# A hand-ordered opening with four projection tiles, and modulation dot products moved out of the gate stage, in an encoder-layer kernel

## The chip, the cores and the metric

The kernel runs on one core of a Trainium2 chip. A core has five engines, each with its own queue, which it works off in order: TensorE (PE in the profile) multiplies matrices into PSUM banks, VectorE (DVE), ScalarE (ACT) and GpSimd (POOL) work on tiles in SBUF, and SyncE (SP) issues most DMAs here. An instruction that waits for a semaphore holds up everything behind it on its own engine. The metric is the device time of one execution in microseconds; lower is better.

## The reference

One layer of an encoder over 1024 tokens of width 1024, in fp32, with one batch element. What is computed:

```python
mod = cond @ w_ada[l] + b_ada[l]                     # cond = silu(c); 6 x 1024 columns
sh1, sc1, g1, sh2, sc2, g2 = jnp.split(mod, 6, axis=-1)
h = modulate(rms_norm(x, norm_mix_g[l]), sh1, sc1)
proj = h @ w_in[l]
q_a, k_a, v_a, qk_m, v_m, o_m, gates = jnp.split(proj, splits, axis=-1)
y_attn = axial_gqa_attention(q_a, k_a, v_a, q_norm_g[l], k_norm_g[l], tables)
y_mem = bidirectional_mlstm(qk_m, v_m, o_m, gates, conv_w[l], conv_b[l], gate_b[l], mlstm_norm_g[l])
mix = jnp.concatenate([y_attn, y_mem], axis=-1) @ w_out[l]
x = x + g1[:, None, :] * mix
h = modulate(rms_norm(x, norm_ffn_g[l]), sh2, sc2)
ffn = (jax.nn.silu(h @ w_gate[l]) * (h @ w_up[l])) @ w_down[l]
x = x + g2[:, None, :] * ffn
```

and a last RMS norm. The attention has 8 query and 2 key heads, the mLSTM 4 heads that run over the sequence in both directions.

## The kernel before

Everything is held transposed: 8 tiles of 128 features by 1024 tokens, in two halves of 512 tokens. Each large product is made of three fp32r matmuls (`mm3`, L297): both factors are split into a high and a low part, and high x high, high x low and low x high are added up. So each weight piece needs a high part (ACT, `whi`) and a low part (POOL, `wlo`), and the input h its `hh` and `hl`.

The stages, in order of time:

1. **Opening.** c is loaded, broadcast to 128 partitions by its DMA, and put through silu (`load_cond`, L364). x is squared and summed (`sum_up`), two matmuls against a tile of ones (L553) give the mean square, and `rstd_steps` takes the root. The modulation `mod` is found in rows of 128: row j of 48 is the dot product of a 128 x 1024 tile of `w_ada` with cond, one DVE instruction (L96, `ada<-ada,cond`) over a tile that a DMA of 512 KB brings. Rows 0 to 7 are the shift and 8 to 15 the scale of the first norm, so the opening needs 16 of them: block k of h needs rows k and 8 + k (`h_steps`). The first three projection tiles (k, v, and the first pair of query heads) are accumulated block by block as h appears. Matmuls of `con` with ones (WARM0 = 9 ahead of the sums, WARM = 6 behind them) are there as well; their result is not used.
2. **Gate stage.** The remaining projections are a list of units, IN (L48): "q" query tiles, "f" tiles of the mLSTM's convolved q and k, "t" chunks with v, o and the gates. `t0` makes the gates; `gate_steps` then computes the mLSTM's decays in a chain of DVE and ACT steps with three visits to TensorE: transposes of the gate rows (`rows`), transposes into columns (`columns`), and one small matmul (`spread`). `rope_steps` (queries and keys) also visits TensorE once per tile, for the squares' sums (`squares`).
3. **Attention** (`scores`, `turned`, `values`), with what is left of IN in the gaps.
4. **mLSTM heads** (`states`, `front`, `back`, `ends`), with the rest of IN and then the output projection (MIX) in the gaps.
5. **Output projection, FFN.**

The order of the instructions on each engine is fixed when the program is built. `Clock` (`ck`) plays the kernel through with estimated costs; a step is emitted at the moment that it would become ready, and a stream of TensorE work is taken when the clock says that its inputs are there (`ck.streams`). `ck.chain` is a row of dependent steps. On the chip each engine then takes its queue in order, whatever the real times.

The other dot products, rows 16 to 47, are made in halves of 512 columns by `ada_late` (64 of them): one load of 256 KB, one DVE instruction. It keeps two tiles (`ahead=2`): the next load waits until the dot before the last one has read its tile. Rows 16 to 39 (48 halves) are to be done by the end of the attention, the last 16 halves during the heads, where a loop makes those that are missing as soon as the units of IN have run out:

```python
        ck.streams(mem, [un], stop=lambda: un.wait is None and all(f.done for v in vo_ok for f in v))
        while not summed:
            ck.need(*adas[-2:])
            ada_late(64)
```

In the gate stage `ready` (L1926) makes up to one half per microsecond, in the attention `scores` one per query block.

## Time and profile before

| | us |
|---|---|
| time, median of 3 runs (lowest, highest) | 1414.26 (1409.74, 1415.05) |
| the profiled execution: its time, its span | 1413.09, 1411.3 |
| busy: TensorE, VectorE, ScalarE, GpSimd | 1304.2, 1074.1, 662.9, 695.8 |
| first projection matmul of the opening | 36.97 |
| first matmul of `t0` (the opening's tiles are done) | 90.91 |
| first score matmul (the attention begins) | 206.24 |
| last `av` matmul (the attention ends), start | 509.3 |
| last transpose of an mLSTM head's output, start | 675.74 |

Times inside the execution are microseconds from the start of the span. L96 is the line of a helper that emits all instructions that `Clock` knows of, and L303 that of the DMA helper; such instructions are told apart by their tiles, `out<-in`. In a timeline row stand the start, the duration, the engine, the line, the operation, the tiles and shapes, and in brackets the idle time of the engine just before, with what ended it. A row of waits gives the total, the number and the longest.

### The profile page before, as it was taken

To read this page: it belongs to the slowest core of one execution; us is meant where nothing else is said; L and a number is where in the kernel's file an instruction comes from. 1 tells how busy PE (TensorE), PEld (TensorE's weight loads), DVE (VectorE), ACT (ScalarE), POOL (GpSimd) and SP (SyncE) were. 2 spreads that over 40 slices of the span, in tenths; PEclk is the share of its full clock that TensorE was granted. 3 is DMA by queue.
4 is the path that set the end of the run, shared out by engine and by line. 5 is a ranking of instruction groups with operands and counts; after the bars stand their busy time and mean duration, and the time that the engine had idled before them with its cause. 6 is when DMAs were issued, how large, how long until landed. Compare 5 with 4: busy or idle time off the path is not lost.

```text
span 1411.3 us, 19469 instructions
## 1 busy us (share of the span) xinstructions
PE 1304.2 (92%) x6594; PEld 1075.1 (76%) x6602; DVE 1074.1 (76%) x1590; ACT 662.9 (47%) x1194; POOL 695.8 (49%) x565
## 2 busy tenths in 40 slices
PE   5789798999999989899996899999999999989997
PEld 2578677889877979777774688888888887767887
DVE  6947979987788848768599886676666654998866
ACT  5454316676666655454575333233333333444462
POOL 5555554545344426687405454545445445545542
PEclk8899999999999999999997899999999999989999
DMA  7536462322122146563551342323322248823324
GB/s 283 168 118 205 132 180 79 101 83 64 38 57 77 34 137 209 180 213 118 192 194 60 101 138 95 107 99 111 113 94 85 83 164 322 297 82 103 92 64 153
DMA packets 103172, 184.39 MB, mean 131 GB/s; under 512 B 11297, under 2 KB 32673, under 8 KB 103073
## 3 DMA queue, kind: packets, MB, share of 16 engines
q1 hardware_dynamic: 89968, 161.06, 35.6%
q10 hardware_dynamic: 13104, 22.10, 4.2%
q8 instruction: 52, 0.85, 0.2%
q14 instruction: 48, 0.39, 0.1%
HBM read 136.19 MB, written 43.25 MB: 127 GB/s over the span
## 4 chain that ended last, share of the span: by engine, by line
PE 58%; DVE 21%; DMA 7%; issue 5%; ACT 4%; POOL 3%; SPq 1%; DVEq 0%; ACTq 0%; POOLq 0%
PE acc L299 14%; PE acc L300 14%; PE acc L298 14%; DVE x L96 3%; DVE ada L96 3%; DVE sst L96 3%; PE av L1029 3%; DMA wst<-act_d 2%; PE T L1010 2%; DVE PT L96 2%; DVE y L96 2%; PE S L978 2%; PE acct L298 1%; PE acct L300 1%; PE acct L299 1%
## 5 line engine op out<-in xcount | busy, mean ns | idle before, releaser
L96 POOL TENSOR_TENSOR wlo<-wst,whi 128x512 fp32r<-128x512 f32 (+2 forms) x190 | 271.0, 1432 | 293.6 <-ACT whi L96 284.3
L96 ACT ACTIVATE whi<-wst 128x512 fp32r<-128x512 f32 (+2 forms) x219 | 131.5, 605 | 131.2 <-POOL wlo L96 25.3
L96 POOL TENSOR_SCALAR P<-P,sst 128x1024 f32<-128x1024 f32 x64 | 88.8, 1391 | 143.7 <-DVE sst L96 114.9
L299 PE MATMUL acc<-x,whi 128*128 128x512 f32 x352 | 140.8, 400 | 6.1 <-DVE x L96 6.1
L96 POOL TENSOR_TENSOR wlo<-wr,whi 128x512 fp32r<-128x512 f32 x60 | 82.3, 1372 | 87.2 <-ACT whi L96 76.7
L298 PE MATMUL acc<-hh,whi 128*128 128x512 f32 x224 | 98.0, 438 | 12.7 <-ACT hh L96 10.2
L96 ACT ACTIVATE P<-S,sst,colq 128x1024 f32<-128x1024 f32 x64 | 77.2, 1207 | 52.4 <-DVE sst L96 49.5
L299 PE MATMUL acc<-hl,whi 128*128 128x512 f32 x224 | 93.1, 416 | 8.4 <-POOL hl L96 4.7
L298 PE MATMUL acc<-whi,wch 128*128 128x512 f32 x244 | 97.2, 398 | 3.9 <-ACT wch L96 3.9
L300 PE MATMUL acc<-whi,wcl 128*128 128x512 f32 x244 | 97.2, 398 | 2.8 <-DVE wcl L96 2.8
L299 PE MATMUL acc<-wlo,wch 128*128 128x512 f32 x244 | 97.5, 399 | 0.8 <-POOL wlo L96 0.7
L96 DVE SCALAR_TENSOR_TENSOR ada<-ada,cond 128x512 f32<-128x512 f32 (+1 forms) x79 | 81.7, 1042 | 18.3 <-DMA ada<-in_w_ada_dram 12.7
L300 PE MATMUL acc<-hh,wlo 128*128 128x512 f32 x224 | 92.0, 411 | 0.0
L96 DVE TENSOR_TENSOR sg<-acc,sg 128x512 f32<-128x512 f32 x67 | 45.4, 687 | 59.9 <-PE acc L300 59.5
L96 ACT ACTIVATE whi<-wr 128x512 fp32r<-128x512 f32 x60 | 37.9, 632 | 111.3 <-DVE wr L96 52.0
L96 ACT ACTIVATE PT<-T 128x512 fp32r<-128x512 f32 x128 | 71.4, 597 | 39.3 <-PE T L1010 38.6
L96 DVE TENSOR_TENSOR PT<-T,PT 128x512 fp32r<-128x512 f32 x128 | 82.8, 681 | 8.0 <-ACT PT L96 7.9
L299 PEld LDWEIGHTS acc<-x,whi 128*128 128x128 f32 x352 | 66.9, 190 | 22.9 <-DVE x L96 7.9
L298 PE MATMUL acct<-whi,hh 128*128 128x256 f32 (+1 forms) x256 | 79.5, 311 | 2.6 <-ACT xp L96 1.2
L1010 PE MATMUL T<-con,P 128*128 128x128 f32 x512 | 71.0, 278 | 9.8 <-DVE PT L96 7.1
L96 DVE TENSOR_TENSOR wcl<-wd,wch 128x512 fp32r<-128x512 f32 x50 | 50.9, 1031 | 38.0 <-ACT wch L96 28.8
L96 DVE TENSOR_REDUCE sst<-S 128x1 f32<-128x1024 f32 x64 | 77.6, 1213 | 2.4 <-PE S L978 2.2
(457 smaller groups left out, 3807.5 us busy)
## 6 DMA issues: line engine op xcount, KB each, us to landing
wr<-in_w_gu_dram SPq DMA_DIRECT2D x66, 256.0 KB, 2.7
ada<-in_w_ada_dram SPq DMA_DIRECT2D x64, 256.0 KB, 3.4
wd<-in_w_d_dram SPq DMA_DIRECT2D x22, 512.0 KB, 6.6
wst<-in_w_gu_dram SPq DMA_DIRECT2D x34, 256.0 KB, 3.1
wst<-act_d SPq DMA_DIRECT2D x33, 256.0 KB, 4.7
ada<-in_w_ada_dram SPq DMA_DIRECT2D x16, 512.0 KB, 5.5
wst<-in_w_o_dram SPq DMA_DIRECT2D x32, 256.0 KB, 3.7
act_d<-sg ACTq DMA_DIRECT2D x31, 256.0 KB, 2.2
```

The costliest lines, as they stand in the source:

```text
L96: return fn(*args, **kw)
L298: nc.tensor.matmul(acc, w[0], x[0], start=first, stop=False)
L299: nc.tensor.matmul(acc, w[0], x[1], start=False, stop=False)
L300: nc.tensor.matmul(acc, w[1], x[0], start=False, stop=last)
L978: nc.tensor.matmul(sp[:, halves(n)], qs[:, j * P:(j + 1) * P], k2[g][m][:, halves(n)], start=m == 0, stop=m == 1)
L1010: nc.tensor.transpose(tp[:, k], Pt[q][:, (4 * b + k) * P:(4 * b + k + 1) * P], ident)
L1029: nc.tensor.matmul(av, va[:, k, h // 4], PT[it][m][:, k], start=(k, m) == (0, 0), stop=(k, m) == (NJ - 1, 1))
```

## The change

- **Opening.** c is loaded as one row into a zeroed tile (`crow`), put through silu as one row, and broadcast by two matmuls with ones. The squares are taken on full tiles, added in pairs on DVE, and summed by eight matmuls. From `dot(8)` on, DVE, ACT and POOL instructions are written out in a fixed order, not left to the clock. POOL's part is only the low halves of weights; all low halves of h are on DVE. Four tiles are made (NT0 = 4, with the second query pair), whose eight weight pieces are loaded into four staging tiles more (`spare`, in the place of the keys). The last block goes tile by tile, so that the first tile is complete first. Then IN has no ("q", 1).
- **Dot products.** `ready` makes none, so none lies between the opening and the attention. By the end of the attention 32 halves are made instead of 48, and 32 instead of 16 fall to the heads; rows 32 to 39 and `sc2` move there with them.
- **Pauses.** `later(dt)` holds a chain back by dt in the planner's time: 2.5 ahead of `squares`, 6.0 ahead of `columns`, 5.0 ahead of `spread`. TensorE gets other work ahead of these steps.

```diff
-WARM = 6
-WARM0 = 9
-POOLED = (0,)
+WARM = 5
+WARM0 = 3
+NT0 = 4
-IN = ([("t", 0), ("q", 1), ("q", 2), ("q", 3), ("f", 0), ("f", 4), ("f", 1), ("f", 5), ("t", 2), ("f", 2), ("f", 6),
+IN = ([("t", 0), ("q", 2), ("q", 3), ("f", 0), ("f", 4), ("f", 1), ("f", 5), ("t", 2), ("f", 2), ("f", 6),
...
+        gp.memset(crow, 0.0)
+        nc.sync.dma_start(crow[0:1], c)
+        for k in range(KT):
+            nc.sync.dma_start(x_t[k], xT[k])
...
+        for j in (8, 0):
+            ada_load(j)
+        for f in range(NT0):
+            first_load(0, f)
+        for j in (9, 1, 10):
+            ada_load(j)
+        nc.sync.dma_start(con, cons)
+        for f in range(NT0):
+            first_load(1, f)
...
+        ac.activation(crow[0:1], crow[0:1], AF.Silu)
...
+        for n in range(NH):
+            nc.tensor.matmul(cb[n], ones, crow[:, halves(n)], start=True, stop=True)
...
+        dot(8)
+        gain(0)
+        root_v(0)
+        root_y(0)
+        ac.activation(msp[0], ry[0], AF.Square)
+        first_hi(0, 0)
+        first_lo(0, 0, gp)
+        dot(0)
+        shift(0)
...
+        def prepare(k):
+
+            if k + 1 < KT:
+                if k > 1:
+                    ada_load(9 + k)
+                ada_load(k + 1)
+            dot(8 + k)
+            gain(k)
+            dot(k)
+            shift(k)
             for n in range(NH):
...
+                xr(k, n)
+                h_hi_of(k, n)
+            for n in range(NH):
+                h_lo_of(k, n)
+            if k < 5:
+                first_hi(1, k - 1)
+                first_lo(1, k - 1, gp)
...
+        def later(dt):
+
+            def wait():
+                ck.fin = ck.now + dt
+            return wait
...
-            ck.chain(0.0, lambda: evac(0), lambda: evac(1), swap, squares)
+            ck.chain(0.0, lambda: evac(0), lambda: evac(1), swap, later(2.5), squares)
...
-                     lambda: exps(0), lambda: exps(1), state, lambda: exps(2),
+                     lambda: exps(0), lambda: exps(1), state, lambda: exps(2), later(6.0),
                      *[lambda i=i, b=b: columns(i, b) for i in range(2) for b in range(2)],
-                     lambda: dve.tensor_scalar(cols[:, :, 1], cols[:, :, 1], QK, None, op0=OP.mult), decay, spread,
+                     lambda: dve.tensor_scalar(cols[:, :, 1], cols[:, :, 1], QK, None, op0=OP.mult), decay, later(5.0), spread,
...
-        def ada_late(last=48, ahead=2):
+        def ada_late(last=32, ahead=2):
...
-                mod_sum(40, 48)
+                mod_sum(32, 48)
+                dve.scalar_tensor_tensor(sc2, mod[:, 32:40], 1.0, V("norm_ffn_g", 0, KT), op0=OP.add, op1=OP.mult)
...
-        t_ada = [0.0]
-
         def ready():
-            if ck.t > t_ada[0]:
-                ada_late()
-                t_ada[0] = ck.t + 1.0
             return rope_ok[3].done and gates_ok.done and not open_sum[0]
...
-        while len(adas) < 48:
+        while len(adas) < 32:
             ck.need(*adas[-2:])
             ada_late()
...
-        mod_sum(16, 40)
+        mod_sum(16, 32)
```

How this moves instructions is seen in the built programs. On DVE in the opening, one block of h (`x` is the tile of the block, `sq` the root of its half, `sc` the scale, `hh` and `hl` the high and low part of h). Before, for block 3:

```order
L96 TENSOR_TENSOR mod<-modacc,vec 128x1 x2
L96 SCALAR_TENSOR_TENSOR sc_343<-mod,vec 128x1
L96 TENSOR_TENSOR x_242<-x_242,sq 128x512
L96 SCALAR_TENSOR_TENSOR ada,modacc<-ada,cond 128x1024
L96 TENSOR_TENSOR x_242<-x_242,sq 128x512
L96 SCALAR_TENSOR_TENSOR ada,modacc<-ada,cond 128x1024 x2
```

and after the change:

```order
L546 SCALAR_TENSOR_TENSOR ada,modacc<-ada,cond 128x1024
L556 SCALAR_TENSOR_TENSOR sc_270<-modacc,b_271,vec 128x1
L546 SCALAR_TENSOR_TENSOR ada,modacc<-ada,cond 128x1024
L553 TENSOR_TENSOR mod<-modacc,vec 128x1
L609 SCALAR_TENSOR_TENSOR x_233<-x_233,sc_270,sq 128x512 x2
L615 SCALAR_TENSOR_TENSOR hl_215<-x_233,mod,hh_207 128x512 x2
```

A block's two dots now stand ahead of its own steps, the scaling is in the first of them, and the two low parts, which POOL made, have come to DVE.

On DVE after the attention's last `avt`, where the heads begin (`Cs` are the states, `W` the weights of a pair of chunks, `U` and `tr` PSUM banks). Before:

```order
L96 TENSOR_TENSOR mod<-modacc,vec 128x24
L96 TENSOR_TENSOR mod<-mod,modacc 128x24
L96 SCALAR_TENSOR_TENSOR sc_5007<-mod,vec 128x8
L96 SCALAR_TENSOR_TENSOR ada,modacc<-ada,cond 128x512 x3
L96 SCALAR_TENSOR_TENSOR Cs<-Cs,dec,U 128x130 x2
L96 SCALAR_TENSOR_TENSOR W<-tr,W 128x256 x2
L96 SCALAR_TENSOR_TENSOR ada,modacc<-ada,cond 128x512
L96 SCALAR_TENSOR_TENSOR Cs<-Cs,dec,U 128x130 x2
L96 SCALAR_TENSOR_TENSOR W<-tr,W 128x256 x2
L96 SCALAR_TENSOR_TENSOR ada,modacc<-ada,cond 128x512 x2
L96 SCALAR_TENSOR_TENSOR Cs<-Cs,dec,U 128x130 x3
```

and after the change:

```order
L96 SCALAR_TENSOR_TENSOR ada,modacc<-ada,cond 128x512 x2
L96 SCALAR_TENSOR_TENSOR Cs<-Cs,dec,U 128x130 x2
L96 SCALAR_TENSOR_TENSOR W<-tr,W 128x256 x2
L96 SCALAR_TENSOR_TENSOR ada,modacc<-ada,cond 128x512 x2
L96 SCALAR_TENSOR_TENSOR Cs<-Cs,dec,U 128x130
L96 SCALAR_TENSOR_TENSOR ada,modacc<-ada,cond 128x512 x28
L96 TENSOR_TENSOR mod<-modacc,vec 128x16
L96 TENSOR_TENSOR mod<-mod,modacc 128x16
L96 SCALAR_TENSOR_TENSOR sc_5133<-mod,vec 128x8
L96 SCALAR_TENSOR_TENSOR Cs<-Cs,dec,U 128x130
L96 SCALAR_TENSOR_TENSOR W<-tr,W 128x256 x2
```

The units of IN run out soon after the attention (264 chunk matmuls were left to the heads before, 108 are now), the loop quoted above then makes all dots that are missing, and 28 of them stand together between the third and the fourth state update.

Their loads stand together on SP as well (`mq` is a piece of the mLSTM's q, `wst` a weight piece, `x` a piece of the residual). Before, at the same place:

```order
L303 DMA wst<-in_w_o_dram 128x512
L303 DMA v_d_94<-vstg 128x256
L303 DMA mq<-mqk_d_85 128x256
L303 DMA ada<-in_w_ada_dram 128x512 x2
L303 DMA wst<-in_w_o_dram 128x512
L303 DMA mq<-mqk_d_85 128x256
L303 DMA o_d_96<-vstg 128x256
L303 DMA ada<-in_w_ada_dram 128x512 x2
```

and after the change:

```order
L297 DMA ada<-in_w_ada_dram 128x512
L297 DMA o_d_95<-vstg 128x256
L297 DMA ada<-in_w_ada_dram 128x512
L297 DMA wst<-in_w_o_dram 128x512
L297 DMA ada<-in_w_ada_dram 128x512 x26
L297 DMA mq<-mqk_d_84 128x256
L297 DMA x_5493<-in_xT_dram 128x512
```

All other loads of the heads are behind the 26. On TensorE, 150 projection matmuls instead of 129 stand between the transposes of the gate rows and those into columns, and 42 instead of 12 between these and the matmul of `spread`.

More of the change, by code (lines that the diff above doesn't have):

```diff
@@ L583, in layer_kernel @@
[L583 to L611 removed]
+        spare = [kvp.tile([P, S], F32, tag=f"k2{i}", name="spare") for i in range(3)]
```

222 lines of the change are left out of this document (123 added, 99 removed).

## The prediction

> **What bounds the kernel now.** I read the span and the chain of work that ended last, then the busy time of each engine in five stretches, then the waits and the timelines inside them.
>
> ```profile
> span 1411.3 us, 19469 instructions
> PE 58%; DVE 21%; DMA 7%; issue 5%; ACT 4%; POOL 3%; SPq 1%; DVEq 0%; ACTq 0%; POOLq 0%
> ```
>
> The profiled execution took 1413.09 us, 1.8 more than its span and 1.2 under the median of 1414.26. TensorE (PE) carries most of the chain, VectorE (DVE) a fifth.
>
> ```profile
> 0.00:91.00 91.00, 60.23 (x179) 37.79 (x180) 66.08 (x96) 45.84 (x71) 47.96 (x34) 0.87 0.57 201
> 91.00:206.00 115.00, 102.40 (x544) 86.92 (x542) 92.45 (x138) 42.45 (x68) 60.33 (x34) 0.94 0.55 165
> 206.00:510.00 304.00, 288.19 (x1873) 252.67 (x1871) 255.68 (x429) 196.75 (x343) 134.26 (x102) 0.99 0.23 67
> 510.00:531.00 21.00, 16.34 (x122) 15.17 (x124) 6.77 (x19) 10.65 (x24) 8.58 (x19) 1.00 0.69 220
> 531.00:676.00 145.00, 136.19 (x780) 115.78 (x787) 112.19 (x253) 72.11 (x190) 103.58 (x130) 0.98 0.56 180
> ```
>
> Columns: length, busy time of PE, weight load, DVE, ACT, POOL, granted clock, DMA share, GB/s. Stretch 1 is the opening, 2 the gates and the first projections, 3 the attention, 4 and 5 the mLSTM heads. Only the opening leaves PE idle for long; from 206 on PE does little but work. So a microsecond of PE idleness removed is worth one at the end, and one added costs one. I therefore count PE work and PE idleness.
>
> ```profile
> 36.97 0.80 PE L298 MATMUL acc<-hh,whi 128*128 128x512 f32 x1 [5.65 <-ACT hh L96]
> 41.49 0.80 PE L299 MATMUL acc<-hl,whi 128*128 128x512 f32 x1 [3.73 <-DVE hl L96]
> 47.01 0.39 PE L298 MATMUL acc<-hh,whi 128*128 128x512 f32 x1
> 47.24 0.40 PE L299 MATMUL acc<-hl,whi 128*128 128x512 f32 x1
> 78.76 0.75 PE L298 MATMUL acc<-hh,whi 128*128 128x512 f32 x1 [4.56 <-ACT hh L96]
> 90.91 0.29 PE L298 MATMUL acct<-whi,hh 128*128 128x272 f32 x1
> 206.24 2.01 PE L978 MATMUL S<-k,qs 128*128 128x512 f32 x8
> ```
>
> A 512-column matmul starts 0.234 us after the last one. Projection work starts in earnest at 41.5, the three opening tiles end at 90.9, the first score matmul is at 206.2.
>
> **Term 1, the opening.** Four tiles instead of three: 48 more matmuls, 48 x 0.234 = 11.2 us, which today come later. The fair mark of before is 90.9 + 11.2 = 102.1.
>
> ```profile
> 1.16 6.79 SPq L303 DMA_DIRECT2D x<-in_xT_dram  x8
> 5.51 1.06 ACT L96 ACTIVATE cond<-cond 128x1024 f32<-128x1024 f32 x1 [2.58 <-DMA cond<-in_c_dram]
> 7.74 9.36 PE L551 MATMUL acc<-con,ones 128*128 128x512 f32 x18 [7.74 <-DMA con<-in_cons_dram]
> 82.46 0.96 POOL L96 MEMSET gI<- 128x1024 f32 x1
> ```
>
> The x loads now queue on SP behind a load that waits for a 1024-wide POOL memset (0.96 us), so they start about 1 us later, but the 512 KB broadcast of c is gone from ahead of them: no net cost. The silu of c ends near 6 (5.5 + 1.06 at the latest 6.6). Behind it PE has 16 fp32 matmuls against ones (2 broadcast, 3 + 3 warming, 8 sums), 1.04 us each (9 took 9.36): 16.6, so both mean squares stand at about 22.6.
>
> ```profile
> 46.13 0.68 DVE L96 TENSOR_TENSOR x<-x,sq 128x512 f32<-128x512 f32 x1
> 46.74 1.22 DVE L96 SCALAR_TENSOR_TENSOR ada<-ada,cond 128x1024 f32<-128x1024 f32 x1
> 50.51 2.31 DVE L96 SCALAR_TENSOR_TENSOR ada<-ada,cond 128x1024 f32<-128x1024 f32 x1
> 52.76 1.76 DVE L96 TENSOR_TENSOR x<-x,sq 128x512 f32<-128x512 f32 x1
> 58.12 0.69 DVE L96 TENSOR_TENSOR x<-x,sq 128x512 f32<-128x512 f32 x1
> ```
> ```profile
> 52.19 1.78 POOL L96 TENSOR_TENSOR hl<-x,hh 128x512 fp32r<-128x512 f32 x1 [0.44 <-ACT hh L96]
> ```
>
> From 46.13 to 58.12 DVE does two blocks: 6.0 us per block, against 18 x 0.234 = 4.2 of PE. DVE paces the loop. The same instruction takes 0.68 us alone and 1.76 beside a POOL subtraction: 1.08 per collision. The Trainium skill, "SBUF — State Buffer", section "SBUF: two separate sides", has DVE instructions with two SBUF inputs and GpSimd instructions exclude each other for a whole instruction. It speaks against this order: 12 weight subtractions of POOL lie beside it, 13 us by the rule and nothing without it; these rows agree with the rule.
>
> After the mean squares DVE has some ten instructions of 0.68 and a dot of 1.22 to the end of block 0, 8 us, with up to four collisions 12: block 0 is done at 33. Each later block is two dots (2.44), four of 0.68 (2.72) and two tiny ones, 5.5 us, beside 24 x 0.234 = 5.6 of PE; one collision in most of the seven makes it 6.6: 46 together. PE needs 5 more, since most of the last 24 matmuls wait for the last block: 33 + 46 + 5 = **84**, a gain of 18. No collision at all gives 30 + 39 + 5 = 74, and 7.6 a block gives 93. I take 84, near the measured pace of 6.0 for less DVE work on small tiles.
>
> **Term 2, the gates.**
>
> ```profile
> PE T L908 <- ACT T L96: 4.5, 1, 4.5
> PE T L922 <- DVE dexp L96: 4.5, 1, 4.5
> PE ms L651 <- ACT sqk L96: 2.1, 2, 1.6
> ```
> ```profile
> 178.00:182.00 4.00, 4.00 (x17) 3.71 (x18) 0.78 (x3) 0.00 (x0) 0.95 (x1) 0.50 0.93 232
> ```
> ```profile
> L96 DVE SCALAR_TENSOR_TENSOR ada<-ada,cond x29: 654/683/2873, 98.6 to 199.1; 128x512 f32<-128x512 f32 x29
> ```
>
> These are the in-order steps that get a pause: 11.1 us of named waits, and after a wait the granted clock is 0.50 for some 4 us. From 90.9 to 206.2 are 115.3 us; the work there is 192 x 0.124 (272 columns at the rate of 512) + 249 x 0.234 + 2 fp32 sums of 1.04 and 32 fp32 transposes of a quarter of that = 92.5, so 22.8 are lost. After the change 150 matmuls (35 us) instead of 129 stand between the gate rows and the first column step, and 42 instead of 12 between the last one and the spread. The 29 dots (29 x 0.69 = 20 us of DVE) also leave this stretch. I keep 6.8 of loss, some two short waits with their slow clock: a gain of **16**, between 8 (only the pauses' waits, partly) and 21.
>
> **Term 3, the dots come back in one heap.**
>
> ```profile
> L1029 PE MATMUL av<-PT,va x16: 276/276/331, 507.5 to 509.3; 128*128 128x256 f32 x16
> ```
> ```profile
> 516.42 0.69 DVE L96 SCALAR_TENSOR_TENSOR ada<-ada,cond 128x512 f32<-128x512 f32 x1 [5.49 <-ACT cond L96]
> 530.65 0.94 DVE L96 SCALAR_TENSOR_TENSOR W<-tr,W 128x256 f32<-128x256 f32 x2 [0.42 <-ACT W L96]
> ```
> ```profile
> L96 DVE SCALAR_TENSOR_TENSOR ada<-ada,cond x15: 677/685/1608, 516.4 to 558.8; 128x512 f32<-128x512 f32 x15
> ```
> ```profile
>   DVE ada L96: 6.0, 2
> ...
> DMA to landing us min/median/max: 2.5/3.7/6.3
> ```
> ```profile
> 675.74 0.60 PE L1874 MATMUL tr<-con,hs 128*128 128x128 f32 x4
> ```
>
> The second pair of rows is of the loads of these dots: who waited for them, and how long they took. Before, 16 dots (these 15 and one at 560) follow the attention, spread among the heads' steps over 44 us. After, 32 do, and 28 of them stand in one row on DVE, ahead of the fourth state update and the second W pair. Each waits for its own 256 KB, and there are two buffers: load n + 2 is issued when dot n has read. A pair costs 0.69 + 0.08 + a landing of 2.5 + 0.2 of hand-overs (an estimate) = 3.47, so 1.73 per dot; nothing else moves in that time, since SP holds its other loads behind the same 26, so I take the shortest landing, not 3.7 (2.3 per dot). First two ready: 1.4 + 26 x 1.73 = 46 us; with 3.7 it is 62.
>
> Who waits: PE's next head transpose needs the bank that the second W pair reads. Ahead of it PE has only 108 short matmuls (12.6 us) and 9 long ones, used up in the first 20 us. So PE stands. Before, W's second pair ends at 531.6, 22 us after the last `av`; now it ends at 20.5 + 46 + 2 = 69.
>
> Then the rest of the heads. Before: 531.6 to 676.3, 145 us. There, 174 chunk matmuls (20 us) lie in the gaps, which after the change were already done in the attention, and 11 dots. PE bound: 145 - 20 = 125. DVE floor: 112 - 8 = 104. Unchanged coupling: 145. I take 125, since PE is 94% busy there. The heads then take 69 + 125 = 194 instead of 167, 27 longer, with 156 x 0.117 = 18.3 of PE work and 6 long matmuls (1.4) fewer in them: 46.7 of new idleness.
>
> The attention itself gets 18.3 of chunk work more and 32 dots where 19 ran (64 - 29 - 16): 13 x 0.69 = 9 on DVE, beside 48 us of DVE slack in that stretch: nothing, at worst 9.
>
> **Sum.** -18 - 16 + 46.7 = +12.7: span 1424, time 1411.3 + 12.7 + 1.8 = **1426 us**, 0.8% over the median.
>
> **Rivals.**
> - *The heap is repaid in the heads* (ends on the other side). If the heads after it run at DVE's floor, 104 instead of 125, the time is 1405. For it: PE has 20 us less to fill in and 28 dots are out of the way. Against: POOL is busy 104 of 145 there too, and in-order steps couple three engines. It decides below 125 - 12 = 113. Chance 0.2.
> - *Collisions eat the opening, or the pauses move no wait.* Opening at 93 and a stage gain of 8 give 1426 + 9 + 8 = 1443; this is also the case in which the change doesn't do what it says. For it: 1.76 against 0.68. Against: the opening's loop has less DVE work per matmul. Chance 0.13.
> - *Landings of 3.7.* The heap takes 62: 1442. Against it: no other load is in flight. Chance 0.12.
> - *The heap doesn't stop PE*, at 0.69 per dot (19 us): 1426 - 27 = 1399. Two buffers and the 6.0 us that two dots already waited speak against it. Chance 0.05.
>
> **How the numbers follow.** The forecast has 0.5, between 1413 and 1438. About 0.5% (7 us) is what a measurement can tell from no change: below 1407 lie the last rival and half of the first, 0.16; between 1407 and 1421 the rest of the first and a third of the forecast, 0.26; above it 0.58. The range takes in the first rival and the middle ones' near sides: 1400 to 1443. The ends of all bounds together (74, 21, 46, 104 and 93, 8, 62, 145) are further apart and need every term to go one way.
>
> **What would show it.** Right: matmuls on `acct` 128x272 start near 84; no wait over 2 us at the column and spread steps; on DVE a row of 28 `ada` dots 1.7 us apart, each ended by a DMA, and PE idle some 45 us beside it, first step after it a `tr`. Wrong: dots 0.7 apart; PE busy in that stretch; the heads after it done in under 113 us; an opening that ends after 93 or before 74; or the attention longer by more than its 18 us of added matmuls.

## The result: 3.2% slower, and the profile after

| | before | after |
|---|---|---|
| median of 4 runs, us | 1413.65 (1409.74 to 1415.05) | 1459.03 (1455.91 to 1462.03) |
| profiled execution, us | 1413.09 (span 1411.3) | 1459.61 (span 1457.7) |
| ratio, 95% interval | | 1.0324 (1.0305 to 1.0344) |

The forecast of 1426 us had the sign right, and the place in part; the size was wrong: 33.7 us of span are missing from its sum, 14.1 of them in the heads behind the row of dots and 10.3 in the gates. The first lines and the chain of waits of the page of after:

```profile
span 1457.7 us, 19464 instructions
...
PE 56%; DVE 24%; DMA 7%; issue 5%; ACT 4%; POOL 3%; SPq 1%; DVEq 0%; ACTq 0%; POOLq 0%
```

VectorE's share of the chain rose from 21 to 24%. The stretches of after, cut at its own landmarks (start of t0, first score matmul, last `av`, last head transpose); columns as in the prediction: length, busy time of PE, weight load, DVE, ACT, POOL, granted clock, DMA share, GB/s.

```profile
0.00:86.20 86.20, 71.20 (x234) 45.40 (x235) 65.97 (x101) 37.35 (x57) 23.32 (x20) 0.98 0.57 206
86.20:195.80 109.60, 100.06 (x545) 85.53 (x544) 75.67 (x87) 41.86 (x66) 56.77 (x37) 0.94 0.46 122
195.80:505.60 309.80, 293.64 (x1979) 260.28 (x1978) 257.09 (x448) 196.87 (x347) 132.24 (x98) 1.00 0.26 76
505.60:718.30 212.70, 140.79 (x741) 115.50 (x748) 128.03 (x303) 79.31 (x204) 103.89 (x144) 0.84 0.48 155
718.30:1457.70 739.40, 703.63 (x3110) 568.55 (x3108) 539.63 (x657) 295.55 (x501) 340.98 (x248) 0.97 0.39 130
```

In the fourth line, the heads, PE is idle for 212.7 - 140.8 = 71.9 us. Before, the same stretch was

```profile
509.30:676.10 166.80, 152.89 (x905) 131.12 (x911) 118.96 (x271) 83.14 (x214) 112.26 (x148) 0.98 0.58 185
```

that is 13.9 idle. So 58.0 us of idleness are new there, where the sum has 46.7. The timeline of VectorE there (start, length, instruction, and in brackets the idle time before it with what ended it):

```profile
528.22 0.35 DVE L96 SCALAR_TENSOR_TENSOR Cs<-Cs,dec,U 128x130 f32<-128x130 f32 x1
529.45 1.79 DVE L96 SCALAR_TENSOR_TENSOR ada<-ada,cond 128x512 f32<-128x512 f32 x1 [0.88 <-DMA ada<-in_w_ada_dram]
...
534.01 0.69 DVE L96 SCALAR_TENSOR_TENSOR ada<-ada,cond 128x512 f32<-128x512 f32 x1 [1.06 <-DMA ada<-in_w_ada_dram]
535.66 0.71 DVE L96 SCALAR_TENSOR_TENSOR ada<-ada,cond 128x512 f32<-128x512 f32 x1 [0.95 <-DMA ada<-in_w_ada_dram]
...
577.42 0.69 DVE L96 SCALAR_TENSOR_TENSOR ada<-ada,cond 128x512 f32<-128x512 f32 x1 [1.30 <-DMA ada<-in_w_ada_dram]
...
578.80 0.74 DVE L96 SCALAR_TENSOR_TENSOR W<-tr,W 128x256 f32<-128x256 f32 x2
```

28 dots in one row, (577.42 - 529.45) / 27 = 1.78 us apart; the forecast had 1.73. After the first two, nearly all take 0.69 to 0.71 and wait about 1.0 for their load. TensorE's longest wait in the same stretch, and two of its windows:

```profile
PE tr L1788 <- DVE W L96: 46.7, 1, 46.7
```
```profile
540.00:560.00 20.00, 0.00 (x0) 0.00 (x0) 7.86 (x23) 0.00 (x0) 0.00 (x0) 0.50 0.48 150
...
700.00:720.00 20.00, 9.45 (x36) 6.49 (x36) 10.97 (x23) 5.72 (x11) 8.88 (x9) 0.74 0.20 66
```

No matmul at all between 540 and 560, as the forecast said: the head transpose waits for the second W pair, and that for the row. The last window is the end of the heads, with PE half idle; the forecast had no loss there. The gates, by PE's waits between t0 and the first score matmul (`xp` is the copy of a convolution tile out of its PSUM bank, `sqk` the squares of a query or key tile):

```profile
PE ms L737 <- ACT sqk L96: 5.9, 1, 5.9
PE acc L292 <- ACT xp L96: 3.7, 2, 2.9
```

The two waits of 4.5 of before are gone. In their place stands one of 5.9, for the squares of a query tile; ScalarE's timeline shows why they came late:

```profile
137.31 0.59 ACT L96 ACTIVATE sqk<-acc 128x512 f32<-128x512 f32 x1
...
140.43 1.28 ACT L96 ACT_TABLE_LOAD   x1
154.39 1.05 ACT L96 ACTIVATE T<-Fr 64x1024 f32<-64x1024 f32 x1 [12.68 <-DVE Fr L96]
155.47 0.69 ACT L96 ACTIVATE qg<-acc,vec 128x512 f32<-128x512 f32 x1
156.06 0.59 ACT L96 ACTIVATE sqk<-acc 128x512 f32<-128x512 f32 x1
```

ScalarE stood 12.7 us at the gates' first exponential (T<-Fr), which waits for VectorE's scans and the steps behind them. The second half of the tile was queued behind it.

The opening, by VectorE's last instruction of a block (two halves of `hl` together):

```profile
37.29 1.42 DVE L615 SCALAR_TENSOR_TENSOR hl<-x,mod,hh 128x512 fp32r<-128x512 f32 x2
43.99 1.41 DVE L615 SCALAR_TENSOR_TENSOR hl<-x,mod,hh 128x512 fp32r<-128x512 f32 x2
...
64.12 1.41 DVE L615 SCALAR_TENSOR_TENSOR hl<-x,mod,hh 128x512 fp32r<-128x512 f32 x2
72.88 1.42 DVE L615 SCALAR_TENSOR_TENSOR hl<-x,mod,hh 128x512 fp32r<-128x512 f32 x2
```

6.7 us a block, 6.6 was forecast. One block took 72.88 - 64.12 = 8.76.

### The profile page after: what moved, and what is told of

Read it like the earlier page. It is cut to its first block, busy times and chain, and to the rows that moved or that the text cites. A ratio compares the mean times of both kernels' runs of the same rounds, so it can differ in the third digit from the quotient of the medians.

```text
span 1457.7 us, 19464 instructions
## 1 busy us (share of the span) xinstructions
PE 1309.3 (90%) x6602; PEld 1075.3 (74%) x6610; DVE 1066.4 (73%) x1595; ACT 650.9 (45%) x1173; POOL 657.2 (45%) x546
## 4 chain that ended last, share of the span: by engine, by line
PE 56%; DVE 24%; DMA 7%; issue 5%; ACT 4%; POOL 3%; SPq 1%; DVEq 0%; ACTq 0%; POOLq 0%
PE acc L293 14%; PE acc L294 14%; PE acc L292 14%; DVE sst L96 4%; DMA ada<-in_w_ada_dram 3%; DVE y L96 3%; DVE PT L96 2%; DVE x L96 2%; DVE ada L96 2%; PE av L1116 2%; PE T L1097 2%; PE S L1065 1%; DVE ada L546 1%; PE acct L292 1%; PE acct L293 1%
## 5 line engine op out<-in xcount | busy, mean ns | idle before, releaser
L96 POOL TENSOR_TENSOR wlo<-wst,whi 128x512 fp32r<-128x512 f32 (+2 forms) x182 | 260.7, 1439 | 354.3 <-ACT whi L96 342.8
L96 ACT ACTIVATE whi<-wst 128x512 fp32r<-128x512 f32 (+2 forms) x211 | 126.4, 605 | 120.9 <-PE acc L294 24.9
L96 DVE SCALAR_TENSOR_TENSOR ada<-ada,cond 128x512 f32<-128x512 f32 x64 | 52.9, 828 | 38.4 <-DMA ada<-in_w_ada_dram 30.2
L96 POOL TENSOR_TENSOR wlo<-s,whi 128x512 fp32r<-128x512 f32 x44 | 60.3, 1372 | 37.5 <-ACT whi L96 37.5
L96 DVE SCALAR_TENSOR_TENSOR x<-acc,mod,x 128x512 f32<-128x512 f32 (+1 forms) x92 | 62.7, 718 | 15.9 <-PE acc L294 15.9
L1097 PEld LDWEIGHTS T<-con,P 128*128 128x128 f32 x512 | 57.4, 140 | 22.0 <-issue 11.0
```

The lines of the kernel that those rows point to most:

```text
L96: return fn(*args, **kw)
L1097: nc.tensor.transpose(tp[:, k], Pt[q][:, (4 * b + k) * P:(4 * b + k + 1) * P], ident)
```

## The experiments

The change has three parts, and each run below is the change, or the kernel before, with one or more of them undone or added: **O** the opening with four tiles, **P** the three pauses, **D** the dots moved out of the gates (none there, 32 by the end of the attention). D undone and P undone are, on the change:

```diff
         def ready():
+            if ck.t > t_ada[0]:
+                ada_late()
+                t_ada[0] = ck.t + 1.0
...
-        def ada_late(last=32, ahead=2):
+        def ada_late(last=48, ahead=2):
...
-        while len(adas) < 32:
+        while len(adas) < 48:
```
```diff
-            ck.chain(0.0, lambda: evac(0), lambda: evac(1), swap, later(2.5), squares)
+            ck.chain(0.0, lambda: evac(0), lambda: evac(1), swap, squares)
...
-                     lambda: exps(0), lambda: exps(1), state, lambda: exps(2), later(6.0),
+                     lambda: exps(0), lambda: exps(1), state, lambda: exps(2),
...
-                     lambda: dve.tensor_scalar(cols[:, :, 1], cols[:, :, 1], QK, None, op0=OP.mult), decay, later(5.0), spread,
+                     lambda: dve.tensor_scalar(cols[:, :, 1], cols[:, :, 1], QK, None, op0=OP.mult), decay, spread,
```

(with the sums of the modulation's columns and `sc2` back at their old places where D is undone).

### Six of the corners

**e1**, O and P (D undone). 

> The change without its third part: opening and pauses as in the change, the dot products made while the gates run and 48 of them done by the attention's end, as before. In the program 12 of the last 16 dots still stand in one row in the heads, since the fill ahead of them runs out early. Theory 'heap' (every dot in the row stops TensorE for about 1.74 us, 48.6 us for 28): the row of 12 costs some 21 us, so the time is 1459 - 28 + 0 to 6 for the dots that share the gates = 1431 to 1437. Rival 'number' (32 dots in the heads are too many for VectorE wherever they stand, 16 are not): the heads go as before, and the time is 1413.7 - 16 - 6 = 1392 to 1398.

**e2**, O alone (D and P undone). 

> The opening alone: no pauses, and the dots as before. In the program 10 of the last 16 dots stand in rows of 4 and 6. Theory 'heap': the opening gains 16 (first t0 matmul near 86), the rows give back 10 x 1.74 = 17: 1413.7 - 16 + 17 = 1415, within 5. Rival 'the opening's gain is kept': 1398. Rival 'the gates lose what the opening gains' (they end at a time that the loads or the rows of the gates set): first S stays at 206, time 1413.

**e3**, P alone (added to the kernel before). 

> The kernel before with the three pauses and nothing else. The order on TensorE has the same counts of matmuls in every stage. Prediction's own step: the two waits of 4.5 and the pair of 2.1 go, with the slow clock behind them: 11 to 16 less, 1398 to 1403. Theory 'the pauses move the wait' (after the change, 5.9 and 3.7 of other waits stood in their place): 5 to 7 less, 1407. Rival 'no wait moves': 1413, the waits at the column and spread steps still 4.5 each.

**e4**, D alone (added to the kernel before). 

> The kernel before with the dots moved and nothing else: none while the gates run, 32 done by the attention's end, 32 in the heads. Only 9 stand in one row now, the other 23 are spread among the steps. Theory 'heap': 9 x 1.74 = 16 more in the heads, and 0 to 8 less in the gates, which lose 29 dots: 1422 to 1430. Rival 'number': 16 more dots of 0.69 to 1.1 in the heads, 11 to 18 more with no single stop of TensorE over 5 us: 1417 to 1432, told apart by the stop. Rival 'the moved dots are free without the row': 1406 to 1413.

**e5**, O and D (P undone). 

> The change without its pauses. The row of dots falls from 28 to 9, since more of the chunk matmuls (240 against 108) are left to the heads and the dots are made between them. Theory 'heap, set by the fill that is left': 19 x 1.74 = 33 less than the change, 0 to 6 given back in the gates: 1426 to 1432. Rival 'the dots cost what they cost wherever they stand': 1459 to 1465.

**e8**, P and D (added to the kernel before). 

> The change without its opening: pauses and moved dots on the kernel before; 9 dots in the row, 240 chunk matmuls left to the heads. If the three parts add up, this is the time of the dots alone less what the pauses alone gain (forecast 1422 to 1430 less 5 to 7: 1416 to 1425). Theory 'the pauses gain only where the gates hold no dots': 10 to 16 under the dots alone. Rival 'the row is the whole loss': within 3 of the run with opening and dots, plus the 16 that the opening gains.

Measured: median, ratio to the kernel before with its interval (against executions of it taken beside each run, so it isn't quite the quotient of the medians), the stages of the profiled execution in us (to the start of t0; t0 to the first S; attention; heads to the last head transpose), idle time of PE in the heads, the longest rows of dots in the heads and the chunk matmuls that the program leaves to the heads (both counted in VectorE's and TensorE's order).

| parts | median | ratio (95%) | opening | gates | attention | heads | idle | rows | left |
|---|---|---|---|---|---|---|---|---|---|
| none | 1413.65 | 1 | 90.9 | 115.3 | 303.1 | 166.8 | 13.9 | 3, 3 | 264 |
| P (e3) | 1409.88 | 0.9969 (0.9958 to 0.9981) | 90.9 | 113.1 | 301.6 | 164.0 | 13.4 | 3, 3 | 264 |
| D (e4) | 1435.49 | 1.0162 (1.0149 to 1.0175) | 90.2 | 106.2 | 308.1 | 192.6 | 38.1 | 9 | 240 |
| P, D (e8) | 1430.36 | 1.0113 (1.0094 to 1.0131) | 91.0 | 100.2 | 308.3 | 192.0 | 37.7 | 9 | 240 |
| O (e2) | 1427.43 | 1.0105 (1.0092 to 1.0118) | 86.6 | 112.6 | 312.3 | 174.7 | 33.1 | 4, 6 | 144 |
| O, P (e1) | 1437.73 | 1.0172 (1.0157 to 1.0187) | 86.5 | 123.3 | 309.8 | 178.3 | 42.5 | 12 | 132 |
| O, D (e5) | 1425.00 | 1.0075 (1.0058 to 1.0093) | 86.3 | 101.4 | 307.2 | 190.8 | 36.4 | 9 | 240 |
| O, P, D | 1459.03 | 1.0324 (1.0305 to 1.0344) | 86.2 | 109.6 | 309.8 | 212.7 | 71.9 | 28 | 108 |

Before the first S the program places 249 long projection matmuls behind t0's start, but 222 in e2 and 201 in e5: for equal work add 27 x 0.234 = 6.3 us to e2's gates and 48 x 0.234 = 11.2 to e5's (112.6).

What follows. e1 and e5 lie within 1 us of the bands of 'heap'; e2 and e4 came out 7 and 5 us above theirs, so 1.74 per dot in the row isn't all that dots in the heads cost. e8 is 5 us above its band, but within 2 of e4 less what P gains alone (1435.5 - 3.8): P and D add up. With O they don't. O with P costs 10 us more than O, although P alone gains 3 to 4; O with D costs 2 less than O, although D alone costs 22. No part alone is slower by more than 1.6%. The table shows where they meet. With O, the pauses make the planner take 48 projection matmuls more ahead of the first S than in e5 (249 against 201); the attention then has fewer of them to fill with and takes chunk matmuls in their place, and 108 are left to the heads instead of 240. The stage of the heads that lets the planner spread the dots ends when those run out; the dots still missing then are made in one row. So the row of 28 is not D's alone: it needs all three parts. In e4 TensorE stops twice beside its row of 9, as PE's waits between 560 and 610 show:

```profile
PE ni L1814 <- DVE num L96: 14.6, 3, 10.8
PE tr L1875 <- POOL hs L96: 8.4, 1, 8.4
```

So e4's rival 'number', which had no stop over 5, is out too.

In e3 both waits of 4.5 are gone, and others stand in their place, as its second theory says, for a gain of 3.8 where it had 5 to 7. PE's waits in its gates:

```profile
PE acc L298 <- ACT xp L96: 4.8, 2, 4.0
PE ms L657 <- ACT sqk L96: 4.0, 3, 2.3
PE T L829 <- DVE gI L96: 2.0, 2, 1.7
```

### The row itself

**e7**, the change with four buffers for the dots of the heads.

```diff
-        ck.tick = lambda: ada_late(64)
+        ck.tick = lambda: ada_late(64, 4)
...
-            ck.need(*adas[-2:])
-            ada_late(64)
+            ck.need(adas[-4] if len(adas) < 64 else adas[-1])
+            ada_late(64, 4)
```

> The change with four buffers for the dots of the heads instead of two, so that four loads of 256 KB are in flight; the row is 27 long and a first group of 4 stands ahead of it. Theory 'landing' (each dot waits for a load issued when the dot two ahead had read): with four in flight the pace falls to 1.74 / 2 = 0.87 per dot, the row to 24 us, the time to 1459 - 24 = 1435. Rival 'bandwidth' (1.74 us for 256 KB is 150 GB/s, a limit of that queue): the pace stays 1.74, the time 1459. Rival 'VectorE itself': 0.69 each at best, row 19, 1430.

1438.31 us, ratio 1.0169 (1.0148 to 1.0189). VectorE's timeline of e7, in the row:

```profile
524.47 0.68 DVE L96 SCALAR_TENSOR_TENSOR ada<-ada,cond 128x512 f32<-128x512 f32 x1
...
530.89 1.74 DVE L96 SCALAR_TENSOR_TENSOR ada<-ada,cond 128x512 f32<-128x512 f32 x1
...
539.37 0.69 DVE L96 SCALAR_TENSOR_TENSOR ada<-ada,cond 128x512 f32<-128x512 f32 x1 [1.29 <-DMA ada<-in_w_ada_dram]
540.03 0.69 DVE L96 SCALAR_TENSOR_TENSOR ada<-ada,cond 128x512 f32<-128x512 f32 x1
540.70 0.69 DVE L96 SCALAR_TENSOR_TENSOR ada<-ada,cond 128x512 f32<-128x512 f32 x1
541.66 0.69 DVE L96 SCALAR_TENSOR_TENSOR ada<-ada,cond 128x512 f32<-128x512 f32 x1 [0.26 <-DMA ada<-in_w_ada_dram]
543.58 0.69 DVE L96 SCALAR_TENSOR_TENSOR ada<-ada,cond 128x512 f32<-128x512 f32 x1 [1.22 <-DMA ada<-in_w_ada_dram]
...
556.74 0.69 DVE L96 SCALAR_TENSOR_TENSOR ada<-ada,cond 128x512 f32<-128x512 f32 x1 [1.67 <-DMA ada<-in_w_ada_dram]
...
558.12 0.75 DVE L96 SCALAR_TENSOR_TENSOR W<-tr,W 128x256 f32<-128x256 f32 x2
```

The row has 27 dots, (556.74 - 524.47) / 26 = 1.24 apart. Four near its head take 1.69 to 1.74 each; the last 17, which take 0.69, are (556.74 - 539.37) / 16 = 1.09 apart instead of 1.78, where the theory had 0.87. The second W pair starts 54.6 us after the last `av` (503.5) instead of 73.2, and the time falls by 20.7; 24 was expected. So theory 'landing' has the mechanism right and its size a little too large; a limit of 150 GB/s in that queue is out.

**c15**, the change with the last chunk unit held back until the attention has ended.

```diff
             for kind, i in order:
+                if (kind, i) == ("t", 3):
+                    yield [held_back]
...
         ck.streams([Stream(values()), Stream(turned()), Stream(scores())], [un])
+        held_back.set(ck, ck.t)
```

> The change itself, with the last chunk unit not given out before the attention ends, so that 192 chunk matmuls are left to the heads instead of 108. In the program the row of 28 dots becomes rows of 4 and 17. Theory 'the row is what is left when the fill runs out': TensorE's stop falls from 48.6 to about 17 x 1.74 = 30, and the heads, 212.7, to 190 to 197 although they hold 10 us more work; 1438 to 1445. Theory on the rest 'floor': from the second W pair that follows the row to the last head, the heads scale with what of them is left, not with fill. Rival 'the row's length doesn't matter, 32 dots do': 1456 to 1462.

1436.37 us, ratio 1.0172 (1.0145 to 1.0199); the heads:

```profile
508.10:698.50 190.40, 145.76 (x839) 123.09 (x838) 134.58 (x303) 79.81 (x207) 104.43 (x144) 0.92 0.55 176
```

84 chunk matmuls more (9.8 us) in the heads, and the heads are 22 us shorter. TensorE's stop beside the row of 17 is 25.0 instead of 46.7 (30 expected); the time is 1.6 us under the band. That row is what was left when the fill ran out: its length follows from the fill, as the first theory says; the rival, 1456 and up, is out. The theory on the rest of the heads can't be read here, since the row of 17 stands behind the second W pair.

**e6**, the change with all 64 late dots in the attention.

```diff
-        def ada_late(last=32, ahead=2):
+        def ada_late(last=64, ahead=2):
...
-        while len(adas) < 32:
+        while len(adas) < 64:
```

> The change with all 64 late dots made during the attention, none in the heads; opening and pauses kept. 32 more dots of 0.69 = 22 us of VectorE lie beside the attention, where it has 48 us of slack. The chunk matmuls run out earlier still (72 left to the heads). Theory 'heap': the 48.6 us stop goes, the attention grows by 0 to 9, and the tail of the heads stays 14 over forecast: 1459 - 47 + 0 to 9 = 1412 to 1421 with a tail of 139 from the second W pair on; 1398 to 1407 if the tail's loss was the heap's doing too. Rival 'the attention has no room': it grows by 22 or more, 1434 and up.

1408.94 us, ratio 0.9970 (0.9955 to 0.9985): 50 us less than the change. Two stages of e6, attention and heads:

```profile
193.40:514.40 321.00, 299.51 (x2016) 266.92 (x2015) 280.07 (x510) 197.42 (x349) 142.19 (x98) 0.99 0.34 100
514.40:669.60 155.20, 131.07 (x714) 107.51 (x713) 105.93 (x241) 77.34 (x202) 101.91 (x144) 0.96 0.51 158
```

The attention grew by 11.2, of which 36 chunk matmuls (4.2) are work; the 32 dots cost some 7 there. The heads fell by 57.5: the row, and some 9 more. The time lies between the two bands of 'heap', for a tail of 139 and for one at the forecast; the tail, from the second W pair on, took 132.2.

### The heads behind the row

**e9**, e6 with c15's edit: 192 chunk matmuls left to the heads instead of 72. 

> The kernel of the run with all 64 dots in the attention, but the last chunk unit (192 matmuls) isn't given out before the attention ends: 192 chunk matmuls are left to the heads instead of 72, 14 us of TensorE work moved from the attention to the heads. Theory 'the heads' tail is a lack of fill' (24 us of idle TensorE in heads of 155, where the kernel before has 14 in 167): the heads grow by only 2 to 6 to some 159, the attention, 321 now, falls by 4 to 14; the time is 1409 less 2 to 10 = 1399 to 1407. Rival 'the tail is coupling of the engines, whatever the fill': the heads grow by the 14 moved, 169, and the time stays at 1409 or rises. Rival 'VectorE paces the attention': it stays 317 to 321 without the fill, and the time rises by 0 to 5.

1415.78 us, ratio 1.0020 (1.0001 to 1.0039). Its attention and heads:

```profile
196.00:520.60 324.60, 291.26 (x1895) 255.88 (x1894) 279.21 (x510) 196.15 (x344) 141.32 (x98) 0.98 0.32 97
520.60:676.70 156.10, 141.91 (x839) 121.90 (x838) 105.70 (x241) 79.09 (x207) 102.91 (x144) 0.99 0.50 161
```

TensorE got 10.8 us more work in the heads, and they grew by 0.9. The heads without dots take 155 to 157 us with 131 us of PE or with 142 (155.2 to 157.0 in the seven runs with 48 to 192 chunk matmuls left), and 159 to 161 with 204 left: PE does not bound them, and the rival by which they grow by all of the 14 us moved is out. In the attention the theory is out: without 14 us of fill it did not get shorter (324.6 instead of 321.0), so here fill was free beside the dots. The rival that VectorE paces it has the direction right; the time rose by 6.8, more than its 0 to 5, and 2.7 of that are in the gates, which had the same order in both runs.

The prediction's own stretch starts later, at the end of the second W pair. From there to the last head transpose:

| runs | chunk matmuls in it | busy time of PE | length |
|---|---|---|---|
| before | some 170, and 12 dots | 136.0 | 144.8 |
| e9, and the runs with 204 left (e10, c14, c16) | some 100 | 124.8 to 126.9 | 136.9 to 139.3 |
| e6, e11, e12, c13, c17, c18 | none | 113.0 to 114.6 | 132.0 to 133.5 |
| after, e7 | none; a row of dots just ahead | 117.7, 120.1 | 139.0, 139.8 |

Here fill does count, but only by about half: e6 has 13.4 us less of PE than e9 and is 7.2 shorter, and 22.7 less than the kernel before and is 12.6 shorter. (That e9's heads as a whole grew by only 0.9 is because their first part, up to the second W pair, took 17.0 us instead of 23.3.) The last line is a second effect: behind a row the same stretch takes 7 us longer than in e6. Some 4 to 7 of that are PE busy longer, with about the same number of matmuls, at a granted clock of 0.93 and 0.92 instead of 0.97. What links this to the row no run shows.

### The gates

All of these have O, and all 64 dots in the attention, so that no row covers the result.

**e11**, the pause ahead of the squares 8.0 instead of 2.5 (`later(2.5)` to `later(8.0)`). 

> All 64 dots in the attention, and the pause ahead of the squares 8.0 instead of 2.5. Before the first S the change has one wait of 5.9 for the squares, with the granted clock at 0.7 to 0.8 behind it; ScalarE stood 12.7 in its queue on the gates' exponential, with the tile's second half behind it. Theory 'the pause is too short for what stands ahead on ScalarE': the wait goes, first S 6 to 9 earlier (184 to 187 from 193), 1400 to 1403. Rival 'another wait takes its place' (the tile's own banks, as the 3.7 before an 'acc' matmul): first S within 2 of 193, 1409.

1414.91, ratio 1.0009 (0.9990 to 1.0027); gates 113.6 (107.1 in e6). The wait for the squares fell to 3.3, and one of 3.1 at the spread step came; the first S, at 200.1, is later than either theory had it.

**e12**, a fourth pause: `inter, later(6.0), lambda: exps(0)` for `inter, lambda: exps(0)`. 

> All 64 dots in the attention, and a fourth pause, 6.0, ahead of the gates' first exponential, so that ScalarE takes the tile's evacuations before it and not after. 24 projection matmuls (5.6 us) more then lie before the first S. Theory 'ScalarE's place in line': the wait of 5.9 for the squares goes, first S at equal work 6 to 9 earlier, that is 190 to 193 with the 5.6 us more; 1400 to 1404. Rival 'the gates' chain on VectorE sets the end of the stage': first S later by 3 to 6, 196 to 199, 1409 to 1413.

1412.01, ratio 0.9990 (0.9974 to 1.0006); gates 116.0, at equal work 110.4. No wait for the squares, but 5.9 at the spread and 4.9 for `xp`.

**c13**, the fourth tile's rotation behind the scans.

```diff
                 ck.chain(arrive, lambda: gps.tensor_mul(sw, sw, rp[1]),
+                         *([later(22.0)] if i == 1 else []),
                          lambda: dve.tensor_mul(qg, qg, rp[0]),
```

> The change with all 64 dots in the attention, and the two rotation products of the fourth tile (qg by rps, qg plus sw; 3.6 us in the change) made behind the scans of the gates instead of ahead of them. TensorE's order has the same counts. Theory 'VectorE's chain through the gates sets the stage, and the fourth tile lengthened it': the scans start some 4 us earlier after t0 (47 now), the wait of 5.9 for the squares falls to 2 or less, first S at 186 to 190 instead of 193 to 196; time 1402 to 1406 from 1409. Rival 'ScalarE's place in line alone': the scans start earlier, but first S stays at 193 to 196, and the time at 1409.

1413.50, ratio 1.0010 (0.9996 to 1.0025); gates 110.3. The scans start at 130.80 instead of 133.17 in the change, and the first S at 196.6. TensorE's waits in the gates of c13:

```profile
PE ms L738 <- ACT sqk L96: 8.6, 2, 6.4
PE acc L292 <- DVE dec L96: 1.6, 1, 1.6
```

**c14**, the same without pauses. 

> The same two products moved behind the scans, in the kernel with the new opening, 64 dots in the attention and no pauses (1400.7). Theory 'VectorE's chain': the waits at the spread and the squares (5.3 and 2.6) fall by 3 to 5 together, first S 183 to 186 instead of 187.9; time 1396 to 1398. Rival 'the wait moves': first S 187 to 189, time 1401.

1400.05, ratio 0.9919 (0.9900 to 0.9939), gates 101.1: the same as e10 below (101.6). The waits at the spread and the squares, 7.9 together, became 9.1.

**c17**, one convolution tile ahead of query tile 3, and **c18**, the same without pauses.

```diff
-IN = ([("t", 0), ("q", 2), ("q", 3), ("f", 0), ("f", 4), ("f", 1), ("f", 5), ("t", 2), ("f", 2), ("f", 6),
+IN = ([("t", 0), ("q", 2), ("f", 0), ("q", 3), ("f", 4), ("f", 1), ("f", 5), ("t", 2), ("f", 2), ("f", 6),
```

> The change with all 64 dots in the attention and one entry of the list of tiles moved: the first convolution tile is projected ahead of query tile 3 instead of behind it. TensorE's counts per stage stay. On ScalarE no half of a query tile stands right behind the gates' first exponential now (before, the second half of tile 3 did, and TensorE's squares waited 5.9 to 6.4 for it). Theory 'phase': that wait goes, the stage from t0 to the first S takes 100 to 103 instead of 107 to 110; time 1401 to 1405 from 1409 to 1413. Rival 'the gates' chain sets the end and any wait only moves': another wait of 4 to 8 in its place, the stage stays at 106 to 111, the time at 1409 to 1414.

> The same without the three pauses. The order has the same 441 and 192 matmuls before the first S as with them, so the two runs differ by the pauses alone. Prediction's step, that the pauses take 10 us of waits and their slow clock away: 8 to 16 slower than c17. Theory 'a pause moves the wait': 0 to 6 slower than c17.

c17: 1408.41, ratio 0.9973 (0.9960 to 0.9985), gates 108.3. c18: 1412.26, ratio 0.9994 (0.9985 to 1.0004), gates 111.0. PE's longest waits there, in c17 first:

```profile
PE ms L737 <- ACT sqk L96: 6.9, 1, 6.9
```
```profile
PE T L994 <- ACT T L96: 7.4, 2, 4.1
```

Four edits in five runs (c18 for the pauses apart), and each time the same wait or another in its place: the stage stayed between 108 and 114 at equal work, where the change's order up to the first S, run in five kernels, gave 106.9 to 109.8. Moving the fourth tile's products or the phase of the tiles did not bring the lost gain back. Between c18 and c17 the pauses alone are worth 2.7 us of the stage and 3.9 of the time, as 'a pause moves the wait' had it, and not 8 to 16.

The wait for the squares doesn't need the new opening. It stands in e4 as well, where the old opening has no dots behind it and no pauses:

```profile
PE ms L651 <- ACT sqk L96: 6.0, 1, 6.0
```

(5.8 in c16). There the pauses took it away: in e8 0.8 of it is left. With the new opening they did not: 2.7 in e5 without pauses, 5.9 in the change.

### What the opening is worth

**e10**, O, no pauses, all 64 dots in the attention. 

> The opening of the change, all 64 dots in the attention, no pauses. The planner then gives 48 fewer projection matmuls (11.2 us) to the gates and leaves 204 chunk matmuls to the heads, with no order written for it. Theory 'lack of fill': heads of some 160 with 14 idle, gates 101 as in the run without pauses: 86 + 101 + 322 + 160 + 738 = 1407 span at most, 1397 where the attention's added 11 us (48 matmuls moved in) fit beside its 32 dots. Rival 'pauses are needed': first S later than 193 at equal work (over 188 here), 1412 and up.

**c16**, the same without O. 

> The kernel before with the dots moved out of the gates and all 64 made in the attention; the opening and the steps without pauses as before. Gates 106 and opening 90 as in the run with the dots alone, attention 315, heads 161, 736 after: 1408 span, 1410. Theory 'the opening keeps its gain when no row covers it': 9 to 10 slower than the same with the new opening (1400.7), that is 11.2 of moved work and 4 of earlier t0 less 6 lost in the gates. Rival 'the gates eat it': within 3 of 1400.7.

e10: 1400.68, ratio 0.9911 (0.9889 to 0.9933). Its first S is at 187.9, so the rival by which pauses are needed is out. c16: 1408.44, ratio 0.9973 (0.9958 to 0.9989). Without a row the opening keeps 7.8 of the 9 to 10 us expected. e10 and c14 are the fastest of the study, some 12 us under the kernel before and 58 under the change.

## Why the prediction was right about the direction and wrong about the size

By its own steps, in us of span; "forecast" is what the sum has for that stretch, behind the heads what its span of 1424 leaves.

| step | forecast | measured | off by |
|---|---|---|---|
| opening ends | 84 | 86.2 | +2.2 |
| t0 to first S | 115.3 - 16 = 99.3 | 109.6 | +10.3 |
| attention | 303.1 + 18.3 - 11.2 = 310.2 | 309.8 | -0.4 |
| last `av` to the end of the second W pair | 69 | 73.9 | +4.9 |
| rest of the heads | 125 | 139.1 | +14.1 |
| behind the heads | 736.5 | 739.1 | +2.6 |

**Term 1** was right in its pace: from block 2 on a block took 6.7 (6.6 forecast), with one colliding dot in each, and PE needed 5 more. That block 0 was done at 33.1 (33 forecast) is partly luck: the mean squares stood at 20.8 instead of 22.6, and block 0 took 12.3 behind them instead of 10.4. The 2.2 are nearly all one block, in which three weight subtractions of 2.0 each stand in a row on POOL; on VectorE a dot took 2.40 instead of 1.22, and the two small instructions of 128x1 took 1.19 and 1.17 instead of 0.22 and 0.16: three collisions where the forecast allowed for one. The Trainium skill, "SBUF — State Buffer", section "SBUF: two separate sides", has one such instruction shut the other out for its whole length; the two 128x1 instructions, five and seven times as long, agree.

**The heap of Term 3** was right in mechanism and nearly in size: a row of 28, each waiting for its own load, PE stopped for 46.7, the first step after it a `tr`. e7 shows the mechanism by changing it. The row started 23.8 us after the last `av` instead of 20.5, and the pace was 1.78 instead of 1.73.

**The rest of the heads failed**, and is the largest part. The step is "PE bound: 145 - 20 = 125 ... I take 125, since PE is 94% busy there". It took a high busy share for a bound and so booked the 20 us of chunk matmuls, which were no longer there, as 20 us saved. PE was 94% busy because the planner fills the gaps of the heads' own steps with chunk matmuls. Take those out, and a good part of the gaps stays: with neither fill nor dots nor a row ahead, six runs took 132.0 to 133.5 from the second W pair on, some 12 less than before and not 20. That is 7 of the 14.1. The other 7 come only where a row stands just ahead (the change and e7), a cost that the prediction put at nothing; its cause stays open. (The Trainium skill, "Perfetto Trace Analysis", section "Identifying the Most-Contended Engine", takes the engine with the highest occupancy for the one to improve, and judges TensorE by its FLOPs and the share of its weight loads rather than of its matmuls. Here that share was 131.1 of 166.8 us, 79%, still the highest in the heads, and e9 shows that TensorE did not bound them.) For the heads as a whole e9 showed it the other way round: 10.8 us of work more, 0.9 longer. "Unchanged coupling: 145" was the reading that the prediction priced and passed over; 139.1 was measured. The rival on the other side, the heap repaid by heads at VectorE's floor of 104, is refuted for the same reason: even with no dots in it, this stretch of e6 takes 132.2. Among the signs that the prediction named for being wrong there is one for a short rest of the heads, under 113, and none for a long one.

**Term 2 failed second.** "I keep 6.8 of loss ... a gain of 16" was read from the gates of before and added to Term 1 as if the stage behind the opening didn't know which opening it had. With the old opening, pauses and moved dots together do gain 15.1 (e8, 100.2), close to the 16; but the pauses that it was ascribed to bring 2.2 alone (e3), and the dots' leaving 9.1 (e4). With the new opening the same edits leave 17.1 of loss (109.6 against 92.5 of work), not 6.8, a gain of 5.7 where the prediction's lowest was 8. Its sign for this term, no wait over 2 us at the column and spread steps, came true, and the gain did not: waits at other steps stand instead. Which property of the new opening costs these 7 to 10 us is not settled: the squares' wait behind the exponential is shown in the trace, but it comes with the old opening too (e4), and no edit that moved it made the stage shorter.

The rivals: landings were 2.6 in the median, not 3.7; the heap did stop PE; the collisions cost 2 beyond the forecast and not 9; and the pauses did move waits, but to other places, which is the half of that rival that came true.

The sign rested on the heap being larger than the two gains, and that held. One more thing the prediction did not see: it books the row of 28 under the moved dots, while the runs show that D alone makes a row of 9, and the rest comes with O and P together, which use up the fill earlier.

## What to carry to other kernels

A busy share of 94% on an engine that a planner fills is no bound: before you count removed fill as time, ask how long the stage takes with none, or run it with more and with less (here about half of the fill came back). Where deferred work is drained at the end of a stage, look at what ends that stage (here the fill running out), since a change far ahead of it, even one that saves time there, can turn spread work into one serial row. And a loss that a pause takes away must be measured behind the opening it will run with; here a wait that an edit shortened came back elsewhere.

## What the runs showed of the hardware

- A row of loads of 256 KB with two buffers moves one per 1.78 us (some 150 GB/s), with four buffers one per 1.09 (some 240 GB/s), while the median time from issue to landing, over the 32 loads of the heads, rose only from 2.6 to 3.5 us. So with two buffers the time to land, and not a rate of the queue, set the pace. The Trainium skill, "DMA: Bandwidth & Descriptors", section "Anatomy of one DMA — SWDGE (gpsimd) path", gives 2.0 us plus the bytes at 436 GB/s for a transfer of another kind of queue: 2.6 for 256 KB, an estimate that the median of 2.6 agrees with.
- In 40 of the 46.7 us in which PE stood still (540 to 580) its granted clock was 0.50, and it was 1.00 in the attention ahead of it.
- The same order up to the first S took between 106.9 and 109.8 us from t0 to there in five kernels, so a difference of 2 us in one stage of one profile says nothing by itself.
